# Input loads issued first with a fourth decay buffer, and the delta rule's state products regrouped

## The chip, the cores and the metric

The kernel runs on one core of a Trainium2 chip. The metric is the device time of one execution in microseconds; three runs of the kernel before took 3664.01, 3666.64 and 3673.23 us, so its median is 3666.64 us. PE is the matrix engine (TensorE), DVE the vector engine, ACT the scalar engine, POOL the GpSimd engine, SP the engine whose queue issues the DMAs; PEld are PE's weight loads.

## The reference

One sequence of 512 latent tokens (x) and 256 context tokens (ctx), 1024 features, goes through a first block of two layers and a second block of two layers. Only the first block is touched:

```python
# layer 0: even_mixer: adaptive norm, conformer conv (31 taps), differential attention
h = rms_norm(x, norm1_g[i]) * (1 + sc1) + sh1   # sc1, sh1 from silu(c) @ ada_w + ada_b
# layer 1: odd_mixer: hyena (long convolution) beside a gated delta rule
filt = (sin(f2*(sin(f1*(z@w1+b1))@w2+b2)) @ w3).reshape(L, order, 2, ch) * decay
filt = filt / sum(abs(filt))                     # one normaliser per order
y = irfft(rfft(u) * rfft(filt2)) + u * skip[order]
# delta rule, per head, direction and chunk of 64 tokens
v_new = u_c - w_c @ s
o = qd_c @ s + a_c @ v_new
s = s * exp(g_last) + kd_c.T @ v_new
```

The hyena filters depend on weights only, so the kernel computes their spectra during layer 0 and parks them in DRAM.

## The kernel before, in words

Weights are streamed from DRAM in blocks of 128 x 1024 float32 and split into a rounded high part and a remainder (`wsplit`, L60 to L75: `whi` on ACT, `wlo` on DVE), so that a product is three PE passes (`mm3`, L87). All DMAs named below are issued by SP, one after the other: an instruction that waits in SP's queue holds all that stand behind it. The order in each engine's queue is set before the kernel runs by a planner that takes the written order as priority among instructions that it reckons ready at that time; so a queue's order can differ from the written order, and it doesn't adapt at run time.

**The head.** `body` (L2059) makes the constants, calls `mods_begin` (L125: loads `cc`, `ada_sel`, `ada_b`), then `even_mixer`. There the generator `hyena_filters` (L730) is stepped between other work. Its first step loads `hy_z`, `w1`, `w2`, `fb` and computes a two-layer sine network (`sine`, L742) into `hid`. Then come the loads of x (L363, four of 512 KB) and ctx (L380, 1 MB). The next step enters `hyena_spectra` (L652), which loads `w3` (L660), four decay tiles of 256 KB (L663) into three buffers (tag `hydec`), and the skip row (L665, 256 KB). After it come the norm statistics of x and ctx (`squares`, L216) and two calls of `mods` (L141): each streams eight 512 KB blocks of `ada_w` (L150, twelve buffers) through PE (L153), copies the sum out (L157), transposes it (L160) and adds a bias (L161), giving the norm's scale and shift. After four of these steps the generator is stepped once more: eight filter tiles (PE L675, DVE L678, ACT L680 and L683, DVE L684), their normaliser (PE L694, DVE L696). Then `norm` (L245, L255, L256) writes `hh` and `hl`, and the first matmuls of the layer (L90 to L92) can run. Further steps of the generator are spread over the following matmuls; for the second order the same lines run again.

**The delta rule.** `odd_mixer` (L774) runs `Delta.step` six times; each is `prep` and then `recur` (L1312), which treats two chunks. Matrix products of the rest of the layer are handed in as `fill()`. Per chunk and over eight chains (two directions d, four heads): PE L1324 `wT @ S` into a PSUM tile, DVE L1326 `vn`; per direction PE L1333 `kd.T @ vn`, POOL L1334 (state times decay), DVE L1335 (add). From the third step on (8 chunks in all) PE also forms the output: for each chain L1339 `qd @ S` and at once L1340 `at @ vn` into the same columns, which ACT L1344 or DVE L1346 then takes out. The PSUM tiles of these lines (tag `rec`) come from a pool of two (`odrps`, L915). One float32 product is two PE instructions.

Of the kernel before, what the change touches and what calls it, by code (L numbers as in the profile page):

```python
# [19 lines left out]
T = 512  # L20
# [331 lines left out]
                                                   op0=ALU.mult, op1=ALU.add)  # L352


def even_mixer(k, xc):
    nc, a = k.nc, k.a
    regs = [(0, T), (T, C)]
    lam0 = 0.8 - 0.6 * math.exp(0.0)

    def load_x():  # L360
        t = k.tmp([128, 8, T], "xl", bufs=1, pool=k.res)
        for i in range(0, 8, 2):
            nc.sync.dma_start(out=t[:, i:i + 2], in_=a["x"][:, i:i + 2])  # L363
        return t

    with ExitStack() as es:
        hp = es.enter_context(ExitStack())
# [8 lines left out]
        with k.pool("hyf") as hy, k.pool("evf", 2, space=PSUM) as fps:  # L376
            fg = hyena_filters(k, fps, hy)
            next(fg)
            xl = load_x()
            nc.sync.dma_start(out=xc, in_=a["ctx"])  # L380
            next(fg)
            with k.pool("evn") as np_:
                rbs = [k.norm_stats([t], [rg], ps, np_)[0] for t, rg in zip((xl, xc), regs)]
# [52 lines left out]
        with k.pool("evp") as pp, k.behind([k.mods(0, kind, mps, pp, 4) for kind in (2, 3, 4)], 2):  # L436
# [64 lines left out]
            for g in range(2):  # L501
                vb = [k.wsplit(a["ev_w_v"][g, kq * 4:kq * 4 + 4].rearrange("k p f -> p k f")) for kq in range(2)]
                for t in range(6):
                    acc = k.tmp([128, 512], "acc", pool=ps, bufs=None)[:, :256]
                    for kt in range(8):
                        s = slice(kt % 4 * 256, kt % 4 * 256 + 256)
# [3 lines left out]
                    s = slice(g * 256, g * 256 + 256)  # L510
# [5 lines left out]

        hp.close()
        mp = es.enter_context(k.pool("evm", side="right"))
        xl = load_x()
        x = [xl, xc]  # L520
        mix = []

# [17 lines left out]
        with k.pool("eva") as pp, k.pool("evaps", 2, space=PSUM) as ps, k.pool("evop", 1, space=PSUM) as op_, k.pool("evgp", 1, space=PSUM) as gp, \  # L540
# [91 lines left out]
            st = [stack(0), stack(1)]  # L632
# [19 lines left out]
def hyena_spectra(k, order, ps, pool):  # L652


    nc, a = k.nc, k.a
    sab = k.tmp([128, 512], "hysab", bufs=1, pool=pool)
    first = True
    raw = k.tmp([128, 1024], "hyw3", bufs=1, pool=pool)
    for p in range(2):
        nc.sync.dma_start(out=raw[64 * p:64 * p + 64], in_=a["hy_w3"][:, order * 1024:(order + 1) * 1024])  # L660
    decs = [k.tmp([128, 512], "hydec", bufs=3, pool=pool) for _ in range(4)]
    for t in range(4):
        nc.sync.dma_start(out=decs[t], in_=a["hy_decay"][t])  # L663
    skip = k.tmp([128, 512], "hyskip", bufs=1, pool=pool)
    nc.sync.dma_start(out=skip, in_=a["hy_skip"][order].partition_broadcast(128))  # L665
    yield None
    w3 = [k.tmp([128, 1024], f"w{i}", F32R, 2, k.wp) for i in ("hi", "lo")]
    k.split(raw, *w3)
    filt = [None] * 8
    for t in range(4):  # L670
        dec = decs[t]
        for d in range(2):
            acc = k.tmp([128, 512], "acc", pool=ps, bufs=None)
            for part in range(2):
                nc.tensor.matmul(acc, k.hid[:, t * 128:(t + 1) * 128], w3[part][:, d * 512:(d + 1) * 512],  # L675
                                 start=part == 0, stop=part == 1)
            f = k.tmp([128, 512], "hyf", bufs=10, pool=pool)
            nc.vector.tensor_tensor(out=f, in0=acc, in1=dec, op=ALU.mult)  # L678
            if first:
                nc.scalar.activation(out=sab, in_=f, func=AF.Abs)  # L680
            else:
                ab = k.tmp([128, 512], "hyab", bufs=1, pool=pool)
                nc.scalar.activation(out=ab, in_=f, func=AF.Abs)  # L683
                nc.vector.tensor_tensor(out=sab, in0=sab, in1=ab, op=ALU.add)  # L684
            first = False
            if d == 1 and t == 0:
                nc.vector.memset(f[0:1], 0.0)
            filt[4 * d + t] = f
        if order:
            yield None  # L690
    if order == 0:
        yield None
    acc = k.tmp([128, 512], "acc", pool=ps, bufs=None)
    nc.tensor.matmul(acc, k.ones, sab, start=True, stop=True)  # L694
    inv = k.tmp([128, 512], "hyinv", bufs=1, pool=pool)
    nc.vector.reciprocal(out=inv, in_=acc)  # L696


    nc.scalar.mul(skip, skip, 1.0 / 512)
    yield None  # L700
    for par in range(2):
        p = []
        for t in range(4):
            s = k.tmp([128, 512], "hys", bufs=2, pool=pool)
            nc.vector.tensor_tensor(out=s, in0=filt[t], in1=filt[4 + t], op=ALU.subtract if par else ALU.add)
            hi = k.tmp([128, 512], "hyshi", F32R, 4, pool)
            lo = k.tmp([128, 512], "hyslo", F32R, 4, pool)
            k.split(s, hi, lo)
            p.append((hi, lo))
        w = k.wsplit(a["hy_lag"][par])  # L710
        for i in range(2):
            eo = []
            for odd in range(2):
                acc = k.tmp([128, 512], "acc", pool=ps, bufs=None)
                for t in range(2):
                    c = odd * 512 + t * 256 + i * 128
                    k.mm3(acc, (w[0][:, c:c + 128], w[1][:, c:c + 128]), p[2 * odd + t], t == 0, t == 1)
                o = k.tmp([128, 512], "hys", bufs=2, pool=pool)
                nc.vector.scalar_tensor_tensor(out=o, in0=acc, scalar=1.0 / 512, in1=inv, op0=ALU.mult, op1=ALU.mult)
                eo.append(o)  # L720
            e, o = eo
            lo_, hi_ = (k.tmp([128, 512], "hyspec", bufs=2, pool=pool) for _ in range(2))
            if par == 0:
                nc.gpsimd.tensor_tensor(out=e, in0=e, in1=skip, op=ALU.add)
            nc.vector.tensor_tensor(out=lo_, in0=o, in1=e, op=ALU.add)
            nc.vector.tensor_tensor(out=hi_, in0=o if par else e, in1=e if par else o, op=ALU.subtract)
            yield (4 * par + i, lo_), (4 * par + 2 + i, hi_)
# [343 lines left out]
class Delta:  # L1071


    H = 4
    order = ((4, 5, 0, 1, 2, 3), (5, 4, 3, 2, 1, 0))
# [236 lines left out]
    def recur(self, st, fill, kd, US, wT, qd, at):  # L1312
# [4 lines left out]
        for j in range(2):  # L1317
            if j or st < 2:
                fill()
            S = self.S  # L1320
# [3 lines left out]
                nc.tensor.matmul(vn_ps[pf[d], hd], wT[:, c, pf[d]], S[:, c], start=True, stop=True)  # L1324
            vn = self.t([128, 4, 128], "vn")
            nc.vector.tensor_tensor(out=vn, in0=US[j], in1=vn_ps, op=ALU.subtract)  # L1326
            Sn = self.t([128, 8, 128], "S", 2)
            for d in range(2):
                c = slice(d * 4, d * 4 + 4)
# [4 lines left out]
                nc.gpsimd.tensor_tensor(out=Sn[:, c], in0=S[:, c], in1=self.egl[:, ch, tl[d], c].unsqueeze(2).to_broadcast([128, 4, 128]), op=ALU.mult)  # L1334
                nc.vector.tensor_tensor(out=Sn[:, c], in0=Sn[:, c], in1=kv, op=ALU.add)  # L1335
            if st >= 2:
                op_ = self.PS(True).rearrange("p (c s) -> p c s", c=4)
                for c, (d, hd) in enumerate(chains):
                    nc.tensor.matmul(op_[pf[d], hd], qd[:, c, pf[d]], S[:, c], start=True, stop=False)  # L1339
                    nc.tensor.matmul(op_[pf[d], hd], at[pf[d], c], vn[pf[d], hd], start=False, stop=True)  # L1340
                for d in range(2):
                    o = self.oacc[pf[d], tl[d]]
                    if st < 4:
                        nc.scalar.copy(o, op_[pf[d]])  # L1344
                    else:
                        nc.vector.tensor_tensor(out=o, in0=op_[pf[d]], in1=o, op=ALU.add)  # L1346
# [712 lines left out]
def body(tc, a):  # L2059
    nc = tc.nc  # L2060
    with ExitStack() as es:
        k = K(tc, a, es)
        mods = ExitStack()
        k.mods_begin(mods.enter_context(k.pool("mods")))
        xcs = ExitStack()
        xc = xcs.enter_context(k.pool("xc")).tile([128, 8, C], F32, name="xc")

        regs = [(0, T), (T, C)]
        k.dram = es.enter_context(k.pool("dram", space=bass.MemoryType.DRAM))
        k.spec = k.dram.tile([2, 8, 128, 512], F32, name="spec")  # L2070
        xl = even_mixer(k, xc)
        x = [xl, xc]
        with k.pool("h1", side="right") as hp:
            hh = hp.tile([128, 8, TC], F32R, name="hh1")
# [176 lines left out]
```

## Time and profile before

| | |
|---|---|
| median of three runs | 3666.64 us |
| profiled execution, its own time | 3669.55 us |
| its span, first to last instruction | 3667.8 us |
| mean granted clock of PE | 0.968 |
| busy share of the span: PE, DVE, ACT, POOL | 93%, 66%, 40%, 18% |
| moved by DMA | 369.30 MB, mean 101 GB/s |

The profiled execution has 1.75 us outside its span and lies 2.9 us above the median. A busy share is an average over stages with different limits, so the head (the first 63 us) and the delta rule's stage (about 1240 to 1580 us) are read by themselves.

### The profile page before, as it was taken

To read this page: it belongs to the slowest core of one execution; us is meant where nothing else is said; L and a number is where in the kernel's file an instruction comes from. 1 tells how busy PE (TensorE), PEld (TensorE's weight loads), DVE (VectorE), ACT (ScalarE), POOL (GpSimd) and SP (SyncE) were. 2 spreads that over 40 slices of the span, in tenths; PEclk is the share of its full clock that TensorE was granted. 3 is DMA by queue.
4 is the path that set the end of the run, shared out by engine and by line. 5 is a ranking of instruction groups with operands and counts; after the bars stand their busy time and mean duration, and the time that the engine had idled before them with its cause. 6 is when DMAs were issued, how large, how long until landed. Compare 5 with 4: busy or idle time off the path is not lost.

```text
span 3667.8 us, 54936 instructions
## 1 busy us (share of the span) xinstructions
PE 3423.6 (93%) x21924; PEld 2825.3 (77%) x21924; DVE 2433.7 (66%) x3995; ACT 1462.7 (40%) x2525; POOL 672.9 (18%) x587
## 2 busy tenths in 40 slices
PE   6896989999998899889999989999999999999999
PEld 3665878888887666567888877767998877777998
DVE  7998876544448856654333676667877676658886
ACT  4213543213226434323223445544444544644443
POOL 0042201102102432311111032022111032012110
PEclk9997999999999999989999999999999999999999
DMA  6243113333333222432223313332333313242333
GB/s 210 88 161 92 41 52 120 117 120 120 116 111 111 84 76 76 122 100 78 95 92 97 107 59 100 98 119 85 103 105 97 115 50 115 78 132 83 102 98 98
DMA packets 156841, 369.30 MB, mean 101 GB/s; under 512 B 19207, under 2 KB 44167, under 8 KB 156200
## 3 DMA queue, kind: packets, MB, share of 16 engines
q1 hardware_dynamic: 156584, 365.79, 31.4%
q8 instruction: 172, 2.82, 0.3%
q14 instruction: 85, 0.70, 0.1%
HBM read 334.27 MB, written 28.31 MB: 99 GB/s over the span
## 4 chain that ended last, share of the span: by engine, by line
PE 34%; DVE 10%; issue 6%; ACT 3%; POOL 2%; DMA 1%; SPq 0%; DVEq 0%; POOLq 0%; ACTq 0%
PE acc L90 11%; PE acc L92 10%; PE acc L91 10%; DVE wlo L74 1%; DMA wraw<-in_w_up_dram 1%; DVE hb L1614 1%; DVE wslo L85 1%; ACT mp L1849 0%; PE acc L1416 0%; PE acc L1415 0%; PE acc L1417 0%; ACT whi L73 0%; DVE xl L2025 0%; DVE ws L1922 0%; POOL hog L1729 0%
## 5 line engine op out<-in xcount | busy, mean ns | idle before, releaser
L73 ACT CAST whi<-wraw 128x1024 fp32r<-128x1024 f32 (+2 forms) x442 | 407.9, 923 | 865.8 <-PE acc L91 691.0
L74 DVE TENSOR_TENSOR wlo<-wraw,whi 128x1024 fp32r<-128x1024 f32 (+2 forms) x438 | 488.2, 1115 | 185.6 <-ACT whi L73 181.3
L90 PE MATMUL acc<-hh,whi 128*128 128x512 f32 (+1 forms) x1024 | 369.3, 361 | 15.1 <-ACT whi L73 8.2
L92 PE MATMUL acc<-hh,wlo 128*128 128x512 f32 (+1 forms) x1024 | 366.0, 358 | 5.8 <-DVE wlo L74 5.8
L91 PE MATMUL acc<-hl,whi 128*128 128x512 f32 (+1 forms) x1024 | 367.4, 359 | 1.3 <-DVE hl L256 0.8
L91 PE MATMUL acc<-hidl,whi 128*128 128x512 f32 (+1 forms) x768 | 275.2, 358 | 3.6 <-DVE hidl L85 3.6
L90 PE MATMUL acc<-hidh,whi 128*128 128x512 f32 (+1 forms) x768 | 275.2, 358 | 0.0
L92 PE MATMUL acc<-hidh,wlo 128*128 128x512 f32 (+1 forms) x768 | 275.1, 358 | 0.0
L341 POOL TENSOR_TENSOR sqr<-relu 128x512 f32<-128x512 f32 (+1 forms) x96 | 130.8, 1363 | 686.5 <-ACT relu L339 677.7
L90 PEld LDWEIGHTS acc<-hh,whi 128*128 128x128 f32 x1024 | 196.7, 192 | 54.3 <-ACT whi L73 11.0
L92 PEld LDWEIGHTS acc<-hh,wlo 128*128 128x128 f32 x1024 | 196.0, 192 | 40.7 <-DVE wlo L74 7.6
L91 PEld LDWEIGHTS acc<-hl,whi 128*128 128x128 f32 x1024 | 197.4, 193 | 35.6 <-DVE hl L256 3.7
L92 PE MATMUL acc<-shh,wlo 128*128 128x512 f32 (+1 forms) x480 | 194.2, 405 | 6.7 <-DVE wlo L74 6.7
L90 PE MATMUL acc<-shh,whi 128*128 128x512 f32 (+1 forms) x480 | 196.0, 408 | 3.5 <-ACT whi L73 3.5
L91 PE MATMUL acc<-shl,whi 128*128 128x512 f32 (+1 forms) x480 | 194.7, 406 | 0.0
L85 POOL TENSOR_TENSOR flo<-fth,fhi 128x512 fp32r<-128x512 f32 x44 | 84.7, 1924 | 530.4 <-ACT fhi L84 505.4
L90 PE MATMUL acc<-fsh,wshi 128*128 128x256 f32 x576 | 164.1, 285 | 4.7 <-ACT wshi L84 4.7
L91 PEld LDWEIGHTS acc<-hidl,whi 128*128 128x128 f32 x768 | 146.1, 190 | 27.2 <-DVE hidl L85 4.0
L91 PE MATMUL acc<-fsl,wshi 128*128 128x256 f32 x576 | 163.7, 284 | 0.0
L90 PEld LDWEIGHTS acc<-hidh,whi 128*128 128x128 f32 x768 | 145.4, 189 | 23.3
L92 PEld LDWEIGHTS acc<-hidh,wlo 128*128 128x128 f32 x768 | 145.4, 189 | 23.0
L92 PE MATMUL acc<-fsh,wslo 128*128 128x256 f32 x576 | 161.7, 284 | 0.0
(684 smaller groups left out, 9098.6 us busy)
## 6 DMA issues: line engine op xcount, KB each, us to landing
wraw<-in_mlp_w_dram SPq DMA_DIRECT2D x128, 512.0 KB, 3.5
wraw<-in_ada_w_dram SPq DMA_DIRECT2D x96, 512.0 KB, 4.0
wraw<-in_w_in_dram SPq DMA_DIRECT2D x58, 512.0 KB, 3.5
wraw<-in_od_w_fm_dram SPq DMA_DIRECT2D x36, 512.0 KB, 3.5
wraw<-in_w_gate_dram SPq DMA_DIRECT2D x72, 256.0 KB, 3.1
wraw<-in_w_up_dram SPq DMA_DIRECT2D x72, 256.0 KB, 3.1
wraw<-in_w_down_dram SPq DMA_DIRECT2D x48, 256.0 KB, 2.7
wraw<-in_w_down_dram SPq DMA_DIRECT2D x32, 320.0 KB, 3.0
```

The source lines that it names most:

```text
L73: nc.scalar.copy(hi, raw)
L74: (eng or nc.vector).tensor_tensor(out=lo, in0=raw, in1=f32(hi), op=ALU.subtract)
L85: (eng or nc.vector).tensor_tensor(out=lo, in0=src, in1=f32(hi), op=ALU.subtract)
L90: nc.tensor.matmul(out, s[0], m[0], start=first, stop=False)
L91: nc.tensor.matmul(out, s[0], m[1], start=False, stop=False)
L92: nc.tensor.matmul(out, s[1], m[0], start=False, stop=last)
L341: nc.gpsimd.tensor_tensor(out=s, in0=r, in1=r, op=ALU.mult)
L1614: nc.vector.tensor_tensor_scan(out=b[:, hd], data0=rst, data1=lf[:, hd], initial=0.0, op0=ALU.mult, op1=ALU.add)
```

## The change

`load_x` becomes a function of its own that `body` calls right after the constants; ctx is loaded next, and only then `mods_begin` runs. The fourth decay tile gets a buffer of the tag `hyf` (ten buffers, used for filter tiles) instead of a turn on one of the three `hydec` buffers. The skip load moves from before the filter tiles to behind them. In `recur` the eight `qd @ S` are written in a row between `wT @ S` and `kd.T @ vn`, the eight `at @ vn` in a row at the old place; the accumulation now starts with the first head of a direction and ends with its last.

```diff
+def load_x(k):
+    t = k.tmp([128, 8, T], "xl", bufs=1, pool=k.res)
+    for i in range(0, 8, 2):
+        k.nc.sync.dma_start(out=t[:, i:i + 2], in_=k.a["x"][:, i:i + 2])
+    return t
...
@@ even_mixer
             fg = hyena_filters(k, fps, hy)
             next(fg)
-            xl = load_x()
-            nc.sync.dma_start(out=xc, in_=a["ctx"])
             next(fg)
...
@@ hyena_spectra
-    decs = [k.tmp([128, 512], "hydec", bufs=3, pool=pool) for _ in range(4)]
+    decs = [k.tmp([128, 512], "hydec", bufs=3, pool=pool) for _ in range(3)] + [k.tmp([128, 512], "hyf", bufs=10, pool=pool)]
     for t in range(4):
         nc.sync.dma_start(out=decs[t], in_=a["hy_decay"][t])
-    skip = k.tmp([128, 512], "hyskip", bufs=1, pool=pool)
-    nc.sync.dma_start(out=skip, in_=a["hy_skip"][order].partition_broadcast(128))
     yield None
...
     if order == 0:
         yield None
+    skip = k.tmp([128, 512], "hyskip", bufs=1, pool=pool)
+    nc.sync.dma_start(out=skip, in_=a["hy_skip"][order].partition_broadcast(128))
     acc = k.tmp([128, 512], "acc", pool=ps, bufs=None)
     nc.tensor.matmul(acc, k.ones, sab, start=True, stop=True)
...
@@ Delta.recur
             nc.vector.tensor_tensor(out=vn, in0=US[j], in1=vn_ps, op=ALU.subtract)
+            if st >= 2:
+                op_ = self.PS(True).rearrange("p (c s) -> p c s", c=4)
+                for c, (d, hd) in enumerate(chains):
+                    nc.tensor.matmul(op_[pf[d], hd], qd[:, c, pf[d]], S[:, c], start=hd == 0, stop=False)
             Sn = self.t([128, 8, 128], "S", 2)
...
             if st >= 2:
-                op_ = self.PS(True).rearrange("p (c s) -> p c s", c=4)
                 for c, (d, hd) in enumerate(chains):
-                    nc.tensor.matmul(op_[pf[d], hd], qd[:, c, pf[d]], S[:, c], start=True, stop=False)
-                    nc.tensor.matmul(op_[pf[d], hd], at[pf[d], c], vn[pf[d], hd], start=False, stop=True)
+                    nc.tensor.matmul(op_[pf[d], hd], at[pf[d], c], vn[pf[d], hd], start=False, stop=hd == H - 1)
...
@@ body
         k = K(tc, a, es)
+        xl = load_x(k)
         mods = ExitStack()
-        k.mods_begin(mods.enter_context(k.pool("mods")))
+        mp = mods.enter_context(k.pool("mods"))
         xcs = ExitStack()
         xc = xcs.enter_context(k.pool("xc")).tile([128, 8, C], F32, name="xc")
+        nc.sync.dma_start(out=xc, in_=a["ctx"])
+        k.mods_begin(mp)
...
-        xl = even_mixer(k, xc)
+        xl = even_mixer(k, xl, xc)
```

## Rows read from the trace of the kernel before

**Rows 1.** Stretches of the head; busy us (instructions) per engine, clock, DMA share, GB/s
```profile
0.00:9.00 9.00, 1.94 (x2) 0.28 (x2) 2.85 (x10) 1.50 (x2) 0.20 (x4) 1.00 0.29 61
9.00:21.00 12.00, 3.74 (x10) 2.17 (x10) 6.99 (x11) 7.53 (x13) 0.00 (x0) 1.00 1.02 346
21.00:33.00 12.00, 7.57 (x17) 3.54 (x17) 9.07 (x21) 5.41 (x11) 1.12 (x1) 1.00 0.40 156
33.00:52.50 19.50, 15.44 (x60) 6.61 (x60) 14.11 (x28) 6.96 (x14) 0.70 (x1) 0.90 0.99 365
```

**Rows 2.** What SP's queue waited for, to 145 us: total us, times, longest
```profile
SPq L663 <- DVE xl L422: 15.7, 1, 15.7
SPq L663 <- DVE hyf L678: 11.1, 1, 11.1
```

**Rows 3.** Order of time, SP's issues: start us, us, line, tile, count
```profile
1.66 0.42 SPq L52 DMA_DIRECT2D c_cc<-in_cc_dram  x1
6.40 2.01 SPq L363 DMA_DIRECT2D xl<-in_x_dram  x4
32.24 0.33 SPq L663 DMA_DIRECT2D hydec<-in_hy_decay_dram  x1
32.61 2.47 SPq L150 DMA_DIRECT2D wraw<-in_ada_w_dram  x5
```

**Rows 4.** Order of time, the head's path to the first matmul of the layer
```profile
5.27 1.94 PE L756 MATMUL acc<-c_hy_z,c_hy_w 33*64 33x512 f32 x2 [5.27 <-DMA c_hy_w<-in_hy_w_dram]
26.89 0.69 DVE L765 TENSOR_TENSOR hyhid<-hyf,hyhid 64x512 fp32r<-64x512 f32 x1
51.43 2.07 PE L694 MATMUL acc<-hysab,ones 128*128 128x512 f32 x2 [1.47 <-DVE hysab L684]
53.44 4.62 PE L153 MATMUL acc<-wraw,cs 128*32 128x512 f32 x32
63.39 0.79 PE L90 MATMUL acc<-hh,whi 128*128 128x512 f32 x1 [3.56 <-ACT whi L73]
```

**Rows 5.** Stretches after the head and of the delta stage, columns as in Rows 1
```profile
80.00:280.00 200.00, 180.34 (x903) 136.72 (x901) 191.25 (x217) 49.66 (x70) 46.66 (x21) 0.94 0.37 124
1340.00:1500.00 160.00, 154.51 (x1430) 110.11 (x1428) 90.60 (x224) 70.23 (x142) 48.82 (x80) 0.99 0.29 87
1500.00:1580.00 80.00, 65.90 (x619) 44.34 (x618) 55.69 (x124) 21.68 (x47) 24.35 (x25) 0.89 0.29 87
```

**Rows 6.** Order of time, PE and PEld in one chunk, and the next chunk's first products
```profile
1345.73 1.71 PE L1333 MATMUL rec<-vn,kd 64*128 64x128 f32 x16
1348.03 0.43 PE L1340 MATMUL rec<-vn,at 64*64 64x128 f32 x2
1348.39 0.19 PEld L1339 LDWEIGHTS rec<-S,qd 128*64 128x64 f32 x2 [0.17 <-issue]
1348.39 0.43 PE L1339 MATMUL rec<-S,qd 128*64 128x128 f32 x2
1353.44 0.50 PE L92 MATMUL acc<-oh,wlo 128*128 128x512 f32 x1
1355.96 1.58 PE L1324 MATMUL rec<-S,wT 128*64 128x128 f32 x16
1357.47 1.13 PE L1184 MATMUL prep<-gu,c_dn_bm 128*128 128x512 f32 x2
```

**Rows 7.** Order of time, the same chunk's DVE and ACT, and the last step's POOL
```profile
1346.92 1.28 DVE L1335 TENSOR_TENSOR S<-S,rec 128x512 f32<-128x512 f32 x2 [1.53 <-PE rec L1333]
1353.55 1.18 ACT L1344 COPY xl<-rec 64x512 f32<-64x512 f32 x2 [8.38 <-PE rec L1340]
1564.53 2.04 POOL L1334 TENSOR_TENSOR S<-S,egl 128x512 f32<-128x512 f32 x2 [12.29 <-PE rec L1339]
```

**Rows 8.** Stretch of 1500 to 1520, columns as in Rows 1
```profile
1500.00:1520.00 20.00, 13.16 (x49) 7.63 (x49) 16.03 (x37) 3.52 (x5) 9.73 (x11) 0.74 0.27 80
```

More of the change, by code (lines that the diff above doesn't have):

```diff
@@ L352, in sqrelu_mlp, with even_mixer @@
                                                    op0=ALU.mult, op1=ALU.add)
-def even_mixer(k, xc):
+def load_x(k):
[3 more added lines that the diff above has]
+    return t
+def even_mixer(k, xl, xc):
     nc, a = k.nc, k.a
@@ L358, in even_mixer @@
     lam0 = 0.8 - 0.6 * math.exp(0.0)
[L360 to L364, printed above, removed]
     with ExitStack() as es:
@@ L518, in even_mixer @@
         mp = es.enter_context(k.pool("evm", side="right"))
-        xl = load_x()
+        xl = load_x(k)
         x = [xl, xc]
@@ L2062, in body @@
         k = K(tc, a, es)
+        xl = load_x(k)
         mods = ExitStack()
-        k.mods_begin(mods.enter_context(k.pool("mods")))
+        mp = mods.enter_context(k.pool("mods"))
         xcs = ExitStack()
         xc = xcs.enter_context(k.pool("xc")).tile([128, 8, C], F32, name="xc")
+        nc.sync.dma_start(out=xc, in_=a["ctx"])
+        k.mods_begin(mp)
         regs = [(0, T), (T, C)]
```

## The prediction, made before the changed kernel was built or run

> **What bounds the kernel now.** I read the stretches first, because the shares over the whole span (PE 93%) hide stages with other limits. In the head the DMAs are saturated from 9 to 21 us and from 33 to 52.5 us, but between them their share is 0.40 [rows 1]. SP's waits say why: for 11.1 us it stood at L663, the fourth decay tile, until the first filter tile (L678) had released one of the three buffers [rows 2]. In order of time that load leaves at 32.24 and the next ada_w blocks right behind it, at 32.61 [rows 3]. By the bytes of [rows 1], the last ada_w block lands near 52.5. The chain then runs: normaliser L694 at 51.43, the last eight ada_w steps L153 at 53.44 (they stand behind L694 in PE's queue), transpose, bias, `hh`, first matmul of the layer at 63.39 [rows 4]. So the head is bounded first by transfers, then by PE's fixed order.
>
> After it, from 80 to 280 us, DVE is the bound (191.25 of 200 us busy), with PE at 180 [rows 5]. In the delta stage, from 1340 to 1500, PE is the bound (154.5 of 160 us), DVE only 90.6 [rows 5]. There one chunk's output products run as pairs, L1339 and L1340 in turn, each pair of instructions starting 0.36 us after the one before, with 0.17 us in which PE's loads wait for nothing shown [rows 6]. From 1347.67 to 1353.44 that is 16 pairs, 5.76 us. The same PE runs 16 instructions of one form in a row, L1324, from 1355.96 until L1184 begins at 1357.47, that is 1.51 us or 0.094 each, and L1333 in 1.71 [rows 6].
>
> **The change, part by part.** The sum is made against the profiled execution, 3669.55 us (span 3667.8 and 1.75 around it), which lies 2.9 us above the median of the runs, 3666.64.
>
> *The inputs first.* Five SP issues (x 2.01 us, ctx 0.64) go ahead of nine small loads, `cc` at 1.66 to the last `fb` [rows 3]. x begins to move near 1.7 instead of 6.4, so its squares and sums are done some 5 us earlier. The small loads pay: 3.15 MB lie before them, at 0.346 to 0.365 MB per us 8.6 to 9.1 us, so `hy_z` lands near 12.5 instead of 5.27 and the sine network begins 7 us later. In the old run that network was done at 27.6 (26.89 and 0.69) [rows 4], 22 us after its start, interleaved with the sums of x, which filled DVE. DVE had 16 us of work between 9 and 33 [rows 1]; with the sums out of the way, I take 15 to 22 us for the network, thus 27.5 to 34.5. So this edit alone is worth between 0 and 7 us lost on the filter path, and helps by up to 5 on the statistics, which were not late. `cc` is late by the same 8.6 us: DVE's two small operations on it (L133, L134) may hold x's sums in DVE's queue until 12 us, where the old ones began; that is no loss against the old run.
>
> *The fourth buffer.* It removes the 11.1 us stand. The ada_w blocks follow the decay tiles with no wait for a filter. Bytes up to the last block: 61 x 9, 346 x 12, 156 x 12 and 365 x 19.5 KB [rows 1] make 13.7 MB, less the skip row 13.4. At 0.365 that is 36.8 us from about 2.5 on, thus 39 instead of 52.5: a bound of 13 us on what the transfers can give. Twelve buffers are there; from the thirteenth block on SP waits for PE's steps, which need `cc` only. If PE's ada_w steps then come as the blocks land, the way from the last of them to the first matmul (58.06, the end of L153, to 63.39: 5.3 us [rows 4]) gives a first matmul near 45, 18 us earlier. If L694 stays ahead of them, the filter path decides: from the network's end at 27.6 to L694 took 23.8 us with the stand inside; less 11.1 that is 12.7, so L694 at 40 to 47, and 12 us from there to the first matmul (51.43 to 63.39): 52 to 59, 4 to 11 us earlier. Ends for the head are thus a loss of 7 (nothing of the stand comes back, and the late network stays) and a gain of 18. I take 11, the upper end of the second case and the stand itself, the nearest row. DVE must follow to keep it, since it bounds the next 200 us: it was busy 33 of the first 52.5 us [rows 1], so it has 19.5 idle us to give. In the second order SP's 15.7 us stand at the same line also goes [rows 2]; DVE was the bound there, so I count 0.
>
> *The skip load.* One 256 KB transfer per order moves behind the filter tiles, past the ada_w blocks. Its reader on ACT (L699) is not on the path to the first matmul unless ACT's queue waits for it ahead of `hh`; bounds 0 and a loss of a landing, some 6 us; I take 0, because the multiplication needs it only after the normaliser.
>
> *The fourth tile in `hyf`.* Ten buffers hold eight filters and this one; no new wait, 0.
>
> *The products in a row.* PE executes the same 256 instructions. A block of 16 pairs costs 5.76 us; in a row, 16 like L1324 1.51 us and 16 at a similar pitch (1.51 to 1.71 for the two rows seen) [rows 6]. That is 3.1 us with one change of form (0.17): 2.5 to 2.7 us saved. No row shows a 64x64 form in a row; the bounds are the pitch of the pairs (0, nothing saved; more than that isn't possible on PE, since the pairs change form at every step) and that of L1324. I take the latter, since L1333 with half the array's rows runs the same. On the other side stands the pool of two tiles: `op_` now holds one of them while the two `kd.T @ vn` need one each, so the second direction waits for the first one's addition or for `op_` to be taken out. PE can put `at @ vn` in between, at the price of two more changes of form, 0.34 us. So 2.1 us are left of a chunk, and with 8 chunks 16.7. Six of the eight lie where PE is the bound; the last two lie on the recurrence itself, where POOL waited 12.29 us for L1339 [rows 7]. There the gain is the same block, taken off the chain. What is late next is DVE's addition (L1335, two in 1.28 us [rows 7]).
>
> A rule of the Trainium skill speaks against this part: "TensorE: Matmul & The Clock Gate", section The mechanism, says that a weight load overlaps matmuls in flight only where its row group differs. In a row of `at @ vn` four heads share one row group, so by it nothing would be saved and the sum would lose its 16.7. L1324's 16 instructions share all rows and still start every 0.094 us although one lasts 0.27 [rows 6], so the row disagrees; I keep it as a rival with a small chance.
>
> Sum: 11 and 16.7 make 27.7; 3669.55 becomes 3641.9, and 2.9 lower on the scale of the median, 3639. I forecast **3640 us**.
>
> **The rivals.**
> *The head is given back.* DVE is 96% busy from 80 to 280 [rows 5]; if the filters' and spectra's work that was done in the head's idle time is pushed into that stage, the earlier start buys nothing. For it: that stage has 9 us of DVE slack only. Against: the head's own 19.5 idle us. Time: 3666.6 less 16.7, 3650.
> *The products give nothing,* because the 64x64 form doesn't overlap in a row, or the planner keeps them apart. For it: no row shows the form. Against: both neighbouring forms. Time: 3666.6 less 11, 3656.
> *Neither does what it says.* The planner makes the queues anew; new waits can appear elsewhere: the second-order loads or the late small loads eat the head's gain, and the products stay beside each other. Time about 3665.
> *Slower: the bank.* With `op_` in one of two tiles, each chunk's second `kd.T @ vn` waits in PE's queue, first for the addition (0.64 us), or, where it gets the other tile, for `at @ vn` and ACT's two copies (1.18 [rows 7]); everything behind it in PE's in-order queue, the layer's matmuls too, stands with it. That is 0.9 to 3.5 us a chunk. Such gaps also let the clock fall: from 1500 to 1520, with PE busy 13.16 of 20 us, the granted clock is 0.74 [rows 8], so part of the time was at the lower level, 1.2 GHz; 5 us of matmuls at half rate lose 2.5. Together up to 6 us in each of 8 chunks, 48, against 27.7: 20 us slower, 3687. It decides from 3.5 us a chunk on. Against: PE has other matmuls in hand in six of the eight.
>
> **How the numbers follow.** Forecast 60%, head given back 15%, no gain by products 9%, neither 8%, slower 8%. The first case has its own range: head 4 to 18, products 12 to 20, so 3628 to 3651. A measurement of this kernel tells about 0.3% (11 us) from no change, thus faster is below 3655.6. Nearly all of the first two cases is faster, and half of the third: 0.78. The fourth and the rest of the third are within the bound: 0.14. Slower 0.08. The range reaches from 3625 (both at their upper ends) to 3660, so the slower case and the fourth stay out, with a little at the low end.
>
> **What would show it.** Right: no wait of SP at L663; DMA share near 1 from 5 us without a dip; first L90 between 45 and 55 and the whole of 80 to 280 shifted by as much; L1339 and L1340 as two rows of 16, some 3.2 us together with no 0.17 us gaps inside; PE still 95% busy up to the last chunk. Wrong: L756 late and L694 later than 51; a first matmul after 58; `at @ vn` at 0.18 us a piece; waits of L1333 on L1335 or L1344 over 1 us in most chunks; or a stage that isn't touched, after 1700 us, that is longer than before.

## The result and the profile after

The changed kernel takes 3644.95 us, the median of 6 runs (3640.44 to 3648.89); the kernel before, on the same chip, 3665.16 us (6 runs, 3662.05 to 3673.23). The ratio is 0.995, with a 95% interval of 0.994 to 0.996: 20 us less. The forecast was 3640 in a range of 3625 to 3660. So the sum came out nearly right, but its two terms didn't: the products gave what was predicted, the head gave nothing.

The profiled execution of after is the lowest of its runs (3640.44), that of before lay 4 us above its median; the two traces therefore differ by 29 us where the medians differ by 20, and times of single stretches are read with that in mind.

Two stretches of the head of after, columns as in [rows 1], and behind them two of [rows 5]:

```profile
21.00:33.00 12.00, 7.25 (x20) 2.28 (x20) 7.86 (x17) 2.81 (x4) 0.81 (x1) 1.00 1.04 403
33.00:52.50 19.50, 14.75 (x52) 5.59 (x52) 13.64 (x25) 7.78 (x15) 0.00 (x0) 0.94 0.73 274
...
80.00:280.00 200.00, 179.00 (x910) 133.13 (x908) 194.01 (x221) 49.02 (x70) 46.50 (x21) 0.97 0.40 134
...
1500.00:1580.00 80.00, 66.01 (x612) 48.13 (x611) 55.05 (x114) 25.70 (x72) 26.75 (x23) 0.80 0.30 92
```

The transfers did what the change wanted: the DMA share between 21 and 33 us is 1.04 where it was 0.40. From 80 to 280 us DVE is the bound as before, 194 of 200 us busy. The list of SP's waits up to 145 us has no line for the decay loads behind a filter any more ([rows 2]); the largest that is left at ada_w is (total us, times, longest)

```profile
SPq L150 <- PE acc L153: 8.6, 2, 5.0
```

The path to the first matmul, in order of time as in [rows 4] (L755, L764 and L693 are L756, L765 and L694 of before):

```profile
16.19 2.08 PE L121 MATMUL acc<-diag,ones 128*128 128x128 f32 x8 [1.67 <-DVE diag L120]
18.20 1.97 PE L755 MATMUL acc<-c_hy_z,c_hy_w 33*64 33x512 f32 x2
...
32.82 0.69 DVE L764 TENSOR_TENSOR hyhid<-hyf,hyhid 64x512 fp32r<-64x512 f32 x1 [1.34 <-ACT hyhid L762]
...
52.79 2.08 PE L693 MATMUL acc<-hysab,ones 128*128 128x512 f32 x2 [3.78 <-DVE hysab L681]
54.79 3.80 PE L153 MATMUL acc<-wraw,cs 128*32 128x512 f32 x24
...
62.98 0.50 PE L90 MATMUL acc<-hh,whi 128*128 128x512 f32 x1 [2.62 <-ACT whi L73]
```

The sine network starts 12.9 us later, where the prediction had 7: its first matmul now stands in PE's queue behind L121, a product of the norm statistics, which ends at 18.27. The network ends 5.9 us later, the normaliser comes 1.4 us later, the first L90 0.4 us earlier. PE waits 3.78 us for DVE's last addition before the normaliser, and the last ada_w steps, whose loads had all been issued by 43.3 us, stand behind it.

The delta rule's last chunk on PE in order of time (L1323 `wT @ S`, L1329 `qd @ S`, L1336 `kd.T @ vn`, L1341 `at @ vn`), against [rows 6]:

```profile
1544.00 1.58 PE L1323 MATMUL rec<-S,wT 128*64 128x128 f32 x16
...
1545.94 1.58 PE L1329 MATMUL rec<-S,qd 128*64 128x128 f32 x16
1547.45 1.16 PE L1336 MATMUL rec<-vn,kd 64*128 64x128 f32 x8
1548.54 1.58 PE L1341 MATMUL rec<-vn,at 64*64 64x128 f32 x16
1550.05 1.16 PE L1336 MATMUL rec<-vn,kd 64*128 64x128 f32 x8
```

The 64x64 form runs in a row as the others do: 16 in 1.51 us from its first start to the next form's, `qd @ S` as well. The planner put `at @ vn` between the two halves of `kd.T @ vn`, as the prediction had allowed for. This chunk is the only one of the eight in which `qd @ S` is one row of 16. In the other seven the planner puts other matmuls between; in the first chunk it comes as four instructions, four single ones and a row of eight, which begins so, with L1307 behind it:

```profile
1330.86 0.60 PE L1329 MATMUL rec<-S,qd 128*64 128x128 f32 x4
```

In three of the eight chunks `at @ vn` comes as two rows of eight.

How long the recurrence takes is read from the list of one line's instructions (count, shortest, median and longest ns, first and last start in us): from the first `wT @ S` to the last start of `at @ vn` or `kd.T @ vn`. Before, two lines, and after, two:

```profile
L1324 PE MATMUL rec<-S,wT x192: 272/273/324, 1242.4 to 1566.0; 128*64 128x128 f32 x192
...
L1340 PE MATMUL rec<-vn,at x128: 269/294/320, 1348.0 to 1575.5; 64*64 64x128 f32 x128
```

```profile
L1323 PE MATMUL rec<-S,wT x192: 272/273/324, 1234.6 to 1545.3; 128*64 128x128 f32 x192
...
L1336 PE MATMUL rec<-vn,kd x192: 272/272/373, 1241.8 to 1550.9; 64*128 64x128 f32 x192
```

333.1 us have become 316.3, that is 16.8 less. The recurrence also starts 7.8 us earlier, but that is not the head's gain: further down, kernels whose head is that of before start it anywhere from 1230.1 to 1242.6.

### The profile page after: what moved, and what is told of

Same layout as the page of the kernel before. It is cut to its first block, busy times and chain, and to the rows that moved or that the text cites. A ratio compares the mean times of both kernels' runs of the same rounds, so it can differ in the third digit from the quotient of the medians.

```text
span 3638.7 us, 54925 instructions
## 1 busy us (share of the span) xinstructions
PE 3395.9 (93%) x21924; PEld 2817.6 (77%) x21924; DVE 2425.0 (67%) x3995; ACT 1463.0 (40%) x2525; POOL 666.6 (18%) x587
## 4 chain that ended last, share of the span: by engine, by line
PE 40%; DVE 14%; issue 7%; ACT 4%; POOL 2%; DMA 1%; SPq 0%; DVEq 0%; POOLq 0%; ACTq 0%
PE acc L90 11%; PE acc L91 11%; PE acc L92 11%; DVE wlo L74 2%; DMA wraw<-in_w_up_dram 1%; DVE wslo L85 1%; DVE hb L1615 1%; ACT whi L73 1%; PE rec L1336 1%; PE rec L1323 1%; DVE xl L2026 1%; ACT mp L1850 1%; DVE ws L1923 0%; DVE oz L829 0%; DVE wlo L85 0%
## 5 line engine op out<-in xcount | busy, mean ns | idle before, releaser
L90 PE MATMUL acc<-hh,whi 128*128 128x512 f32 (+1 forms) x1024 | 365.6, 357 | 12.1 <-ACT whi L73 7.3
L92 PE MATMUL acc<-hh,wlo 128*128 128x512 f32 (+1 forms) x1024 | 362.7, 355 | 4.7 <-DVE wlo L74 4.7
L90 PE MATMUL acc<-hidh,whi 128*128 128x512 f32 (+1 forms) x768 | 275.3, 358 | 0.0
L92 PE MATMUL acc<-hidh,wlo 128*128 128x512 f32 (+1 forms) x768 | 275.1, 358 | 0.0
L90 PEld LDWEIGHTS acc<-hh,whi 128*128 128x128 f32 x1024 | 194.4, 190 | 51.8 <-ACT whi L73 10.2
L92 PEld LDWEIGHTS acc<-hh,wlo 128*128 128x128 f32 x1024 | 193.8, 189 | 38.9 <-DVE wlo L74 6.6
L92 PE MATMUL acc<-shh,wlo 128*128 128x512 f32 (+1 forms) x480 | 193.9, 405 | 6.7 <-DVE wlo L74 6.7
L90 PE MATMUL acc<-shh,whi 128*128 128x512 f32 (+1 forms) x480 | 196.1, 409 | 3.5 <-ACT whi L73 3.5
L85 POOL TENSOR_TENSOR flo<-fth,fhi 128x512 fp32r<-128x512 f32 x44 | 82.6, 1877 | 530.8 <-ACT fhi L84 505.8
L90 PE MATMUL acc<-fsh,wshi 128*128 128x256 f32 x576 | 163.6, 284 | 4.6 <-ACT wshi L84 4.6
L90 PEld LDWEIGHTS acc<-hidh,whi 128*128 128x128 f32 x768 | 145.5, 189 | 23.3
L92 PEld LDWEIGHTS acc<-hidh,wlo 128*128 128x128 f32 x768 | 145.6, 190 | 22.9
L92 PE MATMUL acc<-fsh,wslo 128*128 128x256 f32 x576 | 161.7, 284 | 0.7 <-DVE wslo L85 0.7
```

The costliest lines, as they stand in the source:

```text
L85: (eng or nc.vector).tensor_tensor(out=lo, in0=src, in1=f32(hi), op=ALU.subtract)
L90: nc.tensor.matmul(out, s[0], m[0], start=first, stop=False)
L92: nc.tensor.matmul(out, s[1], m[0], start=False, stop=last)
```

## The experiments

The questions were which of the two parts gave the 20 us, why the head gave none, and whether the products gain by fewer changes of form or by the new place of `qd @ S`. A form is the shape of a product on PE's array: 128x64, 64x128 or 64x64, rows by columns. Times in brackets are those of the kernel before in the same batch.

**1. The products alone.** The change of `recur`, nothing else.

```diff
@@ recur
+            if st >= 2:
+                op_ = self.PS(True).rearrange("p (c s) -> p c s", c=4)
+                for c, (d, hd) in enumerate(chains):
+                    nc.tensor.matmul(op_[pf[d], hd], qd[:, c, pf[d]], S[:, c], start=hd == 0, stop=False)
...
-                    nc.tensor.matmul(op_[pf[d], hd], qd[:, c, pf[d]], S[:, c], start=True, stop=False)
-                    nc.tensor.matmul(op_[pf[d], hd], at[pf[d], c], vn[pf[d], hd], start=False, stop=True)
+                    nc.tensor.matmul(op_[pf[d], hd], at[pf[d], c], vn[pf[d], hd], start=False, stop=hd == H - 1)
```

> The delta rule's regrouping alone; the head as before. Theory A (the gain of the products is what the matrix engine saves by not changing form at each product, some 2.1 us a chunk): the stage from the third step on is 16 us shorter, as in the changed kernel, the start of the first layer matmul stays at 63.4, the total is 14 to 18 us under the kernel before. Rival B (part of that shift came with the earlier head): 8 to 12 us under.

3644.50 us (3662.29), ratio 0.9955 (0.9938 to 0.9971): 17.8 us less.

```profile
L1324 PE MATMUL rec<-S,wT x192: 272/273/323, 1242.6 to 1557.0; 128*64 128x128 f32 x192
...
L1337 PE MATMUL rec<-vn,kd x192: 272/272/373, 1249.8 to 1562.6; 64*128 64x128 f32 x192
```

The recurrence takes 320.0 us here, in a profiled execution (3654.53 us) that lies 10 us above its median. Within the intervals, all that the change gives comes from this part.

**2. The head alone:** loads first, fourth buffer, skip load moved; `recur` as before.

> Everything but the regrouping: loads first, fourth buffer, skip load behind. Theory A: the first layer matmul stays near 63 as in the changed kernel, the shift of 4 to 5 us appears only between 160 and 240 us, the total is 4 to 6 us under the kernel before, a quarter of the whole gain. Rival B (the planner's new queues gave the further shift of 6 us between 1100 and 1320): 9 to 12 us under.

3663.17 us, ratio 0.9998 (0.9988 to 1.0009). The head is worth nothing that can be measured: between 4 us gained and 3 lost, not 11. Theory A's 4 to 6 us are not what the median shows, and rival B's 9 to 12 are outside the interval. The skip load's move was not run by itself.

**3. The fourth buffer alone.**

```diff
-    decs = [... "hydec", bufs=3 ... for _ in range(4)]
+    decs = [... "hydec", bufs=3 ... for _ in range(3)] + [... "hyf", bufs=10 ...]
```

> The fourth decay buffer alone, with the loads in the old order. Theory A (the late small loads eat what the buffer gives): the sine network ends at 27.6 as before, the normaliser matmul moves from 51.4 to 45 to 48, the first layer matmul from 63.4 to 55 to 59; the total is 8 to 12 us under the kernel before, more than with the loads first. Rival B (the filters are paced by the matrix and vector engines and not by the stand): first layer matmul at 61 to 63.5, and only the 4 to 5 us between 160 and 240 us are gained.

3659.84 us, ratio 0.9994 (0.9982 to 1.0006). A stretch, PE in order of time, and DVE in order of time:

```profile
21.00:33.00 12.00, 7.21 (x20) 4.59 (x19) 9.06 (x21) 5.42 (x11) 1.12 (x1) 1.00 1.03 403
```

```profile
49.96 2.07 PE L694 MATMUL acc<-hysab,ones 128*128 128x512 f32 x2 [1.47 <-DMA wraw<-in_ev_w_fm_dram]
51.97 4.91 PE L153 MATMUL acc<-wraw,cs 128*32 128x512 f32 x32
...
62.21 0.79 PE L90 MATMUL acc<-hh,whi 128*128 128x512 f32 x1 [3.57 <-ACT whi L73]
```

```profile
43.46 0.68 DVE L684 TENSOR_TENSOR hysab<-hysab,hyab 128x512 f32<-128x512 f32 x1
44.06 1.29 DVE L705 TENSOR_TENSOR hys<-hyf,hyf 128x512 f32<-128x512 f32 x2
45.26 0.69 DVE L684 TENSOR_TENSOR hysab<-hysab,hyab 128x512 f32<-128x512 f32 x1
45.86 1.29 DVE L85 TENSOR_TENSOR hyslo<-hys,hyshi 128x512 fp32r<-128x512 f32 x2
47.07 0.69 DVE L684 TENSOR_TENSOR hysab<-hysab,hyab 128x512 f32<-128x512 f32 x1
...
49.23 0.68 DVE L684 TENSOR_TENSOR hysab<-hysab,hyab 128x512 f32<-128x512 f32 x1
```

This is the run that decides the prediction's step. The stand of 11.1 us is gone and the transfers are full, the sine network ends at 27.6 as before, and yet L694 comes at 49.96 instead of 51.43: 1.5 us of the 11.1. L694's row names a DMA, but the last addition, at 49.23, ends at 49.91, 0.05 us before L694 starts. By the rows, the last four of the seven additions L684 start about 2 us apart, with the next step's L705 and L85 between them in DVE's queue, and each needs ACT's L683, which has one buffer. PE had finished its filter products by 43. So rival B's times for the head are met, theory A's are not.

**4. The loads first alone.**

> The inputs' loads first alone, three decay buffers. Theory A: sine network done at 33 instead of 27.6, the stand at the fourth decay tile some 6 us later, the first layer matmul at 67 to 70, the total 3 to 7 us over the kernel before. Rival B: first layer matmul within 1 us of 63.4, total unchanged.

3665.01 us, ratio 1.0006 (0.9996 to 1.0016). The network ends at 33.6, the first L90 comes at 65.33, 1.9 us later than before. SP stands 17.5 us at the fourth decay tile here instead of 11.1, and the normaliser is still only 1.5 us later (52.91): the stand grew by 6.4 us and the path by much less. The first L90 lies between the two theories, the total is as rival B has it. That the inputs move first gains nothing measurable, and delays the head a little.

**5. L694 behind the ada_w steps.** With the fourth buffer, and the normaliser's accumulator taken from the pool of the mods' accumulators, so that PE can't run it before the last L153 and its copy.

```diff
-        mps = hp.enter_context(k.pool("evmps", 2, space=PSUM))
+        k.mps = mps = hp.enter_context(k.pool("evmps", 2, space=PSUM))
...
-    decs = [... for _ in range(4)]
+    decs = [... for _ in range(3)] + [... "hyf", bufs=10 ...]
...
-    acc = k.tmp([128, 512], "acc", pool=ps, bufs=None)
+    acc = k.tmp([128, 512], "acc", pool=ps if order else k.mps, bufs=None)
     nc.tensor.matmul(acc, k.ones, sab, start=True, stop=True)
```

> Fourth decay buffer alone, and the normaliser L694 takes its accumulator from the pool of the mods' accumulators, so that PE can't run it before the last ada_w step (L153) and its copy. Theory A, PE's fixed order bounds the head: with the buffer alone the last ada_w load was issued at 44.0 us, but L694 stood ahead of the last eight L153 steps until 49.96. Freed of it, L153 ends near 48, the first L90 comes 5.3 us later, near 53.5 (62.2 with the buffer alone). If that is kept to the end, 8 to 9 us less than before, ratio 0.9977; if DVE, the bound from 80 to 280 us, gives it back, ratio 1.000 with the early L90. Rival B, the filters on DVE and ACT hold the norm too (the bias L161 stands behind the additions L684 in DVE's queue): first L90 at 59 to 62, ratio 1.000.

3663.51 us (3660.53), ratio 1.0005 (0.9995 to 1.0015). PE in order of time, then DVE:

```profile
47.54 1.05 PE L160 MATMUL acc<-c_ada_sel,wraw 128*128 128x4 f32 x8 [2.60 <-ACT wraw L157]
48.53 5.31 PE L153 MATMUL acc<-wraw,cs 128*32 128x512 f32 x32
...
55.46 1.10 PE L694 MATMUL acc<-hysab,ones 128*128 128x512 f32 x2
59.16 1.22 PE L90 MATMUL acc<-hh,whi 128*128 128x512 f32 x2 [2.60 <-ACT whi L73]
...
63.70 0.80 PE L92 MATMUL acc<-hh,wlo 128*128 128x512 f32 x1 [1.89 <-DVE wlo L74]
```

```profile
56.61 3.36 DVE L696 RECIPROCAL hyinv<-acc 128x512 f32<-128x512 f32 x1 [0.79 <-PE acc L694]
59.88 1.31 DVE L256 SCALAR_TENSOR_TENSOR hl<-nt,mods,hh 128x512 fp32r<-128x512 f32 x2
```

PE's order was one of several: the first L90 comes 4.2 us earlier than before, within rival B's 59 to 62 and not at theory A's 53.5, and the ratio is B's too. The second mods' steps L153 start only at 48.53 and take 5.31 us; they stand behind the first one's L160, which waits 2.60 us for ACT's copy L157, and that copy stands behind filter work (L84, L683) in ACT's queue. Most of the 4.2 us is given back at once: the reciprocal of 3.36 us, which used to run beside PE's ada_w steps, now stands ahead of the norm's L256 in DVE's queue, and PE waits at the first L92, which comes 1.6 us earlier than before. Between 80 and 120 us the instructions of DVE and ACT stand 1.1 us earlier than in the trace of before, which is what the buffer alone (experiment 3) shows too; the trace of experiment 7, whose head is that of before, stands 2.5 us earlier there, so 1.1 us is within what traces of one head differ by. Here each freed engine handed the wait to the next queue.

**6. The filters behind the norm.** The generator's loads and first-order filter tiles are written after the norm.

```diff
             nc.sync.dma_start(out=xc, in_=a["ctx"])
-            next(fg)
...
-                        if i == 3:
-                            next(fg)
+                        pass
...
                 k.norm([xl, xc], regs, ...)
+                next(fg)
+                next(fg)
```

> Head only: the generator's loads and the first-order filter tiles are written behind the norm instead of inside the mods, so that the first matmul of the layer waits for transfers and the ada_w steps alone. x, ctx and ada_w are 11.5 MB, at 0.36 MB per us 32 us from about 6 on: last L153 near 39, first L90 at 43 to 47, some 18 us earlier than before. Theory A (DVE sets the end of the stretch up to 280 us, so an early first matmul is given back): the filter work moves into that stretch, ratio 0.999 to 1.002. Rival B (the first matmul's time is kept): 15 to 18 us less, ratio 0.995 to 0.996.

3669.60 us (3661.78), ratio 1.0022 (1.0013 to 1.0031): slower. PE in order of time:

```profile
41.77 3.63 PE L153 MATMUL acc<-wraw,cs 128*32 128x512 f32 x28
...
61.39 0.80 PE L675 MATMUL acc<-whi,hyhid 128*128 128x512 f32 x1 [12.05 <-DVE hyf L678]
...
71.26 0.79 PE L90 MATMUL acc<-hh,whi 128*128 128x512 f32 x1 [0.73 <-ACT whi L73]
```

The ada_w steps end at 45.4 instead of 58.06 (39 was expected), but the first L90 does not follow: the planner put the filter products ahead of it on PE, and those wait up to 12 us for DVE, which writes the norm and the filters in turn. Neither theory's number was met, so the run doesn't tell whether an early first matmul would be kept. It shows again that the order in the queues sets it, not the transfers.

**7. Both products in a row at the old place.** `qd @ S` is not moved: eight of it, then eight `at @ vn`, behind `kd.T @ vn`.

> Delta rule only: eight qd @ S in a row and eight at @ vn in a row, but both at the old place behind kd.T @ vn. Theory A, the gain is the form changes that go: 16 and 16 instructions take 1.34 us each and two changes 0.17 each, 3.0 instead of 5.76, 2.7 us in each of 8 chunks, 21 less: ratio 0.994 to 0.996, as with the products moved. Rival B, the gain comes from where qd @ S now stands (it fills PE while DVE makes vn, and POOL's wait for it goes): then this kernel keeps little of it, ratio 0.998 to 1.000.

3638.47 us (3660.53), ratio 0.994 (0.9927 to 0.9954): 22.1 us less.

```profile
1546.06 1.58 PE L1339 MATMUL rec<-S,qd 128*64 128x128 f32 x16
1547.58 1.58 PE L1341 MATMUL rec<-vn,at 64*64 64x128 f32 x16
1549.08 0.50 PE L92 MATMUL prep<-hyv,wlo 128*128 128x512 f32 x1
```

The block takes 3.02 us where the pairs took 5.76 [rows 6]; 2.74 times 8 chunks is 21.9. So the gain is the changes of form that went, and the new place of `qd @ S` adds nothing. Its recurrence takes 315.0 us (1233.9 to 1548.9). It is 4 us better than the products of experiment 1, but the intervals overlap. Two things in the traces point that way: there `at @ vn` stands between the halves of `kd.T @ vn`, and `qd @ S` is broken up by other matmuls in seven of the eight chunks; here `qd @ S` is one row in seven of eight and `at @ vn` in all. What each is worth was not measured apart.

**8. `at @ vn` in turn with `kd.T @ vn`.** As 1, but each `at @ vn` is written behind the `kd.T @ vn` of its chain.

```diff
                     nc.tensor.matmul(kv[:, hd], kd[...], vn[...], start=True, stop=True)
+                    if st >= 2: nc.tensor.matmul(op_[...], at[...], vn[...], start=False, stop=hd == H - 1)
```

> Delta rule only: qd @ S in a row at the new place, but each at @ vn written right behind the kd.T @ vn of its chain, so that the two forms alternate again. Theory A (form changes): the block of 16 and 16 alternating instructions costs about 5.8 us as the old pairs did, instead of 1.7 + 1.34 + 0.34; 2.4 us a chunk are lost again, 19 of the 17.8 gained: ratio 0.999 to 1.001. Rival B (place of qd @ S): the gain stays, ratio 0.995 to 0.996.

3653.45 us (3660.53), ratio 0.9978 (0.9966 to 0.999): 7.1 less than before, so about 10.7 of the 17.8 are lost, between the two theories. In the trace, at a granted clock of 1.00 from 1350 to 1352.5 us:

```profile
1350.88 0.48 PE L1337 MATMUL rec<-vn,kd 64*128 64x128 f32 x2
1351.29 0.43 PE L1339 MATMUL rec<-vn,at 64*64 64x128 f32 x2
1351.65 0.48 PE L1337 MATMUL rec<-vn,kd 64*128 64x128 f32 x2
...
1353.61 1.66 PE L1339 MATMUL rec<-vn,at 64*64 64x128 f32 x10
```

Where the forms alternate, a change costs what it did in the old pairs: 0.77 us for two of each form, 0.385 a step against 0.36 [rows 6]. This also settles a rival: in the old pairs the second product adds into the columns that the first has just written, and that could have been what cost the time; here the two forms write different tiles, and the price is the same. The second direction's `at @ vn` got into a row of ten, in all eight chunks, so about half the changes are back, and a little more than half of the gain is lost.

**9. Everything that looked useful in the head, with the products:** the fourth buffer, L694 behind the ada_w steps, products as in 1.

> The products as in the changed kernel, the fourth buffer, the loads in the old order, and L694 behind the ada_w steps. Theory A (the order of PE bounds the head, and what the head gains is kept): 17.8 and 8 less than before, ratio 0.993, 7 us faster than the products alone. Rival B (the head gains nothing or is given back): ratio 0.9955, as the products alone.

3645.44 us (3660.53), ratio 0.9955 (0.9942 to 0.9968), as the products alone, which is rival B.

**10. The filters behind the norm, with 7.**

> The filter work behind the norm, as in the run before, and the delta rule's products in a row at the old place (qd @ S behind kd.T @ vn). Theory A (the head is given back): ratio 0.993 to 0.995, as the products alone. Rival B (it is kept): 0.989 to 0.990.

3645.76 us (3661.78), ratio 0.996 (0.9948 to 0.9972): about 6 us worse than 7, as experiment 6 alone was worse than before.

**11. The two directions in turn.** As 1, but `at @ vn` goes through the heads with both directions for each.

```diff
-                for c, (d, hd) in enumerate(chains):
-                    nc.tensor.matmul(op_[pf[d], hd], at[pf[d], c], vn[pf[d], hd], start=False, stop=hd == H - 1)
+                for hd in range(H):
+                    for d in range(2):
+                        nc.tensor.matmul(op_[pf[d], hd], at[pf[d], d * 4 + hd], vn[pf[d], hd], start=False, stop=hd == H - 1)
```

> As the products alone, but at @ vn is written with the two directions in turn, so that neighbours use different rows of the array. Theory A (in a row of one form the start of the next instruction doesn't depend on its rows): 0.084 us from one instruction to the next in runs of either kind, 1.34 us for 16. Rival B (a weight load overlaps only where its rows differ): the alternating runs are faster than the 0.084 us seen with the same rows.

One run, 3638.04 us, so its time is not compared. Here, and for comparison in the changed kernel:

```profile
1548.86 1.09 PE L1343 MATMUL rec<-vn,at 64*64 64x128 f32 x16
1549.88 0.82 PE L1337 MATMUL rec<-vn,kd 64*128 64x128 f32 x5
```

```profile
1336.32 1.08 PE L1341 MATMUL rec<-vn,at 64*64 64x128 f32 x8
1337.34 1.16 PE L1336 MATMUL rec<-vn,kd 64*128 64x128 f32 x8
```

Sixteen of both directions in turn take 1.02 us, and eight of one direction take the same 1.02. Theory A falls: the two directions, which use different rows of the array and, as their outputs lie in different partitions, different columns, run side by side. Sixteen in the written order took 1.51, because the second direction, which started 0.49 us after the first, ran beside its last part only.

**12. All four products in turn, at the old place.**

```diff
+            alt = [(d * 4 + hd, d, hd) for hd in range(H) for d in range(2)]
-            for c, (d, hd) in enumerate(chains):
+            for c, d, hd in alt:
                 nc.tensor.matmul(vn_ps[pf[d], hd], wT[:, c, pf[d]], S[:, c], start=True, stop=True)
...
+            kvs = [self.PS(True).rearrange("p (c s) -> p c s", c=4) for d in range(2)]
+            for c, d, hd in alt:
+                nc.tensor.matmul(kvs[d][:, hd], kd[pf[d], c], vn[pf[d], hd], start=True, stop=True)
...
+                for c, d, hd in alt:
+                    nc.tensor.matmul(op_[pf[d], hd], qd[:, c, pf[d]], S[:, c], start=hd == 0, stop=False)
+                for c, d, hd in alt:
+                    nc.tensor.matmul(op_[pf[d], hd], at[pf[d], c], vn[pf[d], hd], start=False, stop=hd == H - 1)
```

> Delta rule only: the order of the kernel with both products at the old place, and in all four products (wT @ S, kd.T @ vn, qd @ S, at @ vn) the two directions in turn instead of one after the other, so kd.T @ vn has both PSUM tiles open at once. Theory A (the instructions of the two directions use different rows or columns of the array and run side by side, each direction at 0.109 us from start to start): 16 take 1.02 us instead of 1.51, 0.49 less in 4 products of 8 chunks and 2 products of 4 chunks, 40 times, 20 us less than the 22 of that kernel: ratio 0.988 to 0.990. Rival B (both tiles open make PE wait, or the stage's end is set by DVE and POOL): ratio 0.993 to 0.996.

3621.71 us (3660.43), ratio 0.989 (0.9873 to 0.9906): 38.7 us less than before. It beats the changed kernel, whose interval ends at 0.994.

```profile
L1325 PE MATMUL rec<-S,wT x192: 272/273/324, 1234.6 to 1533.0; 128*64 128x128 f32 x192
...
L1343 PE MATMUL rec<-vn,at x128: 269/269/321, 1337.2 to 1541.2; 64*64 64x128 f32 x128
```

```profile
1534.76 1.16 PE L1331 MATMUL rec<-vn,kd 64*128 64x128 f32 x16
...
1539.39 1.09 PE L1341 MATMUL rec<-S,qd 128*64 128x128 f32 x16 [1.87 <-DVE S L1337]
1540.42 1.09 PE L1343 MATMUL rec<-vn,at 64*64 64x128 f32 x16
```

The recurrence takes 306.6 us. `kd.T @ vn` differs between the directions in rows only, `qd @ S` in columns only, `at @ vn` in both; in turn, all three take 1.0 to 1.1 us for 16. Two open tiles make PE wait at `qd @ S` for DVE's addition, here 1.87 us and 3.7 us in all three such places: rival B's mechanism is there, at a small price. The step from 7 to 12 is 17 us against the 20 expected.

## Why the prediction came out as it did

**The products: right, in mechanism and size.** 16.7 us were forecast, 17.8 measured for this part alone (11 to 23 by the interval). The unknown pitch of the 64x64 form was taken from its neighbour L1324 and was the same, 1.51 us for 16. The sum for a block was loosely made: 1.51, 1.51 and 0.17 are 3.2 and not 3.1, which leaves 2.6 us saved and 2.2 after the two more changes of form. Those were foreseen; that `qd @ S` would be broken up by other matmuls was not.

**The rule on weight loads: dismissed too quickly.** I kept the rule of the Trainium skill ("TensorE: Matmul & The Clock Gate", section The mechanism) that a weight load overlaps matmuls in flight only where its row group differs as a small rival, because L1324's 16 start every 0.094 us. That mean hides two streams. In the single starts of the changed kernel's trace, matmuls of one direction follow each other at 0.109 us, and the two directions overlap for part of the time. Matmuls of one row group do follow each other faster than one of them lasts (0.27 us), so products in a row of one group did gain here, and the rule as I applied it stays wrong for the sum. But what lies in other rows or columns does run beside it, and that was worth another 17 us. The Trainium skill says so in "TensorE: Matmul & The Clock Gate", section Why this matters for your kernels: matmuls in distinct row groups or with outputs at distinct column groups run concurrently. Experiments 11 and 12 agree, with 1.02 us for 16 instead of 1.51.

**The head: wrong.** The step that failed is "from the network's end at 27.6 to L694 took 23.8 us with the stand inside; less 11.1 that is 12.7, so L694 at 40 to 47". Most of the stand was not inside: 11.1 us that end at 32.24, with the second filter product and not the first, began at 21.1 [rows 2] [rows 3], so only 4.7 of them lie behind the network's end at 27.6. And taking all of it away gave 1.5: with the stand gone and the network unchanged (experiment 3) that way took 22.4 us. The wait on SP was long, but lay beside the path and not on it: what L694 waits for is DVE's chain of multiplications and additions, with ACT and other DVE work between. Taking 11.1 us off was the error of reading a wait as a delay. In the changed kernel the network ends at 33.5, within the forecast 27.5 to 34.5, because it took the 15 us at the low end while its start came 12.9 us later and not 7. L694 comes at 52.79, outside. L694 after 51 and a first matmul after 58 (62.98) were the prediction's own signs of being wrong. The rival "the head is given back" has the head worth nothing, as measured, but for another reason: there was nothing to give back at first; where PE did come earlier (experiment 5), 2.7 of the 4.2 us were gone by the first L92. Whether a first matmul at 45 to 52 would be kept to the end was not shown, since no kernel got there.

**The bank: a rival that stayed small.** `kd.T @ vn` waits for the bank only 0.5 us in the whole changed kernel, in a trace in which the planner put `at @ vn` between the halves; so the 0.9 to 3.5 us a chunk did not come. The clock from 1500 to 1580 us did fall, to 0.80 from 0.89 [rows 5], but the recurrence, 25 us earlier, now ends well inside that stretch, so the two hold different work.

**Sum.** 27.7 us were forecast and 20.2 measured; 16.7 against 17.8 for the products, 11 against nothing (4 less to 3 more, experiment 2) for the head. The range held because it reached to the case in which the head gives nothing. That the time lies within 5 us of the forecast is luck: it lies as near to the 3650 of the rival, and only the runs of each part tell the two apart.

## What to carry to other kernels

Group products of one shape, and inside a group alternate those that use different rows or different columns of the array; here the first was worth 22 us and both together 39. Before a long wait of a queue is taken off the time, follow the path from its end: if the instructions that it feeds stand behind something else at the same moment, the wait is free. Look also at when the wait began and ended: only the part that lies inside an interval can come off it. And where several in-order queues interleave two jobs, freeing one queue moves the wait to the next; look for the last queue, not the longest wait.

## What the runs showed of the hardware

The same small matmuls cost, by their order alone, 0.19 us each where two forms alternate (0.77 for four, experiment 8), 0.13 in a row of eight of one direction (1.02, the change of form included) and 0.064 with both directions in turn (1.02 for 16). The Trainium skill, "TensorEngine Tiling (Array Packing)", section Key Properties, says that changing the tiling mode drains the engine and that different tiles work in parallel; these rows agree with both and give the sizes.

One trace also shows the clock falling under a busy PE: in experiment 8 the granted clock from 1340 to 1360 us is 0.67, with PE busy all of the 20 us and 19.62 of the 20 before (at 0.92), so the engine was part of the time at its lower level, 1.2 GHz.

```profile
1340.00:1360.00 20.00, 20.00 (x92) 13.73 (x90) 7.51 (x11) 4.37 (x8) 5.93 (x10) 0.67 0.10 37
```

What made it fall there was not settled. The recurrence of that single trace takes 335.1 us (1230.1 to 1565.2), more than the 333.1 of before, though the median is 7.1 us lower; so the recurrence of one trace measures a gain only roughly.
